# Unread identity products on TensorE ahead of the first weights and at eleven places of block 1

## The chip, the cores and the metric

One Trainium2 chip, of which the kernel uses one core. The metric is the device time of one execution in microseconds (us). PE is the tensor engine, DVE the vector engine, ACT the scalar engine, POOL the general engine (GpSimd), SP the engine that issues the transfers (DMAs).

## The reference

Two blocks in a row over one sequence of 256 tokens, model width 1024, in float32. The first:

```
def first_block(x, ...):
    h = rmsnorm(x, norm1_g)
    hp = h @ w_in
    y_ssm = s5_mixer(hp[..., :o1], ...)
    y_nsa = nsa_mixer(hp[..., o1:o2], hp[..., o2:o3], hp[..., o3:o4], ...)
    gate = sigmoid(hp[..., o4:].reshape(bsz, s, 2, 1024))
    merged = gate[..., 0, :] * (y_ssm @ w_proj_ssm) + gate[..., 1, :] * (y_nsa @ w_proj_nsa)
    x = x + merged @ w_out
    h2 = rmsnorm(x, norm2_g)
    return x + square(relu(h2 @ w_up)) @ w_down
```

`s5_mixer` is a diagonal complex recurrence of 32 groups of 16 channels with 64 states each, a skip term, GELU and a gated projection. `nsa_mixer` is attention of 8 heads of width 64 in 2 key groups, with three branches that gates add up: attention to keys and values of compressed blocks of 32 tokens, to selected blocks of 64, and to a window of 512. At 256 tokens the selection (16 blocks) and the window take in all earlier tokens. The second block has two layers, each a half-weighted gated feed-forward, a mixer (retention in the one, latent attention in the other, both with attention to a memory), and a feed-forward. The change touches the first block alone.

## The kernel before

The class `Prog` issues the program piece by piece on a tile framework. The framework gives out buffers, puts in the waits, and decides itself in which order the instructions of each engine stand; only an instruction given to `keep_in_program_order` keeps its place. So the order of the program's text is a wish, and a few more instructions at one place can move others elsewhere.

Activations lie transposed, 128 channels by 128 tokens, in two token tiles t = 0 and 1 (`xT`). Weights come from HBM in blocks of up to 1024 KB a transfer (`raw`), issued by SP. Most are split in two halves (`load`, L262 and L263): ACT rounds to `wh`, DVE subtracts to get `wl`, and three products of the fast kind (fp32r, one pass of the array) stand for one f32 product. Some matrices of block 1 (the inputs of the recurrence `u`, queries `q`, keys and values `kvb` and `kva`, the first quarter of the gates `mg`) are multiplied unsplit (`raw_proj`, L304) as f32, for which PE makes two passes: a count of x8 in the trace is four such products. Their blocks land in turn in the buffers named `raw`, `wh` and `wl`, so `mm<-wh,hTl` with eight in a group at the beginning is such a product, too.

`mm` (L222) issues every matrix product, `tr` (L226) every transpose, which is a product with the identity `idn`. All results land in eight banks: two called `tr`, two `mm`, and `acc0` to `acc3`. A new owner of a bank waits for the last reader of the one before.

Block 1 weaves four strands together (0 to about 185 us):

- `block1_proj` (L879 on), once per token tile: the projections above, and for q and k the norm of each head (`head_norm`: DVE sums up `nms` L854 and L855, POOL takes it to the power −1/2 as `nr` L332 and multiplies `q` L858), then transposes in `flip` (`u_rest`, `q_rest` L911, `c_rest` L931, `k_rest` L947). After them come the gates `mg`.
- the recurrence: `ssm_setup` makes its tables, among them `K0` by 32 small products of 32 columns; then eight steps `ssm_states` (L765 to L780): products of `uT` and `sB` into acc0 and acc1, four multiplications on DVE by the table `cst` (L765, into `ta` and `tb`), two sums (L766, L767), a scan (L775), a rotation back (L776, L777), and POOL's part (L779, L780). From the third step on POOL makes the table `cst` itself (`ssm_table`, L743 to L745). `ssm_out` multiplies the states by `sC`.
- the compressed attention: `compress`, which makes the compressed keys and values (`ph`, then `kc`) and the weights `PcT` of both token tiles (L1030 on).
- the heads: `nsa_pair` (L1060 on), one pair of heads c (g = 0 and 1) at a time: scores into acc2 and acc3, maximum and exponential (L1074, L1076), then the scaling `ns` by `nsm` (L1088 on DVE for t = 0, L1086 on ACT for t = 1), the transposes of `ns`, and a copy to `PT` (L1095), from which `nsa_values` makes the output.

Behind block 1's mixers come the feed-forward and the second block, which are large products from end to end.

Of the kernel before, what the change touches and what calls it, by code (L numbers as in the profile page):

```python
# [15 lines left out]
P = 128  # L16
# [161 lines left out]
class Prog:  # L178
# [42 lines left out]
    def mm(self, out, l, r, start, stop, **kw):  # L221
        self.nc.tensor.matmul(out, l, r, start=start, stop=stop, **kw)  # L222
# [73 lines left out]
    def raw_proj(self, out, name, n, hT):  # L296

        _, _, K, _, uk, un = MATS[name]
        nk = K // P
        for kb in range(nk // uk):  # L300
            w = self.raw_unit((name, n, kb))
            for k in range(uk):
                kk = kb * uk + k
                self.mm(out[:, :un], hT[:, kk], w[:, k, :], kk == 0, kk == nk - 1)  # L304
            yield
# [29 lines left out]
    def consts(self):  # L335
        nc, cp = self.nc, self.cp
        self.idn = self.sb(cp, [P, P], "idn")
        make_identity(nc, self.idn)
        self.mhalf = self.sb(cp, [P, 16], "mhalf")
# [231 lines left out]
    def ssm_setup(self, pool, np_):  # L571
        nc, v, g = self.nc, self.nc.vector, self.nc.gpsimd
# [9 lines left out]
        sp = sb([P, 48], "sp")  # L582
# [49 lines left out]
        g = nc.gpsimd  # L632
# [68 lines left out]
        pt = self.ps("tr")  # L701
        for i in range(4):
            for n in (0, 1):
                for jj in range(4):
                    j = 4 * i + jj
                    self.mm(pt[32 * jj:32 * jj + 32, 32 * i:32 * i + 32], bs[n][:, j, :], self.sC[:, 0, n, j, :], n == 0, n == 1, tile_position=(0, 32 * jj))
# [162 lines left out]
    def block1_proj(self, sp, pool, t):  # L869
# [16 lines left out]
        def flip(src, n):  # L886
            pt = self.ps("tr")
            for c in range(n):
                self.tr(pt[:, c * P:(c + 1) * P], src[:, c * P:(c + 1) * P])
            return pt  # L890
# [50 lines left out]
        def k_rest(k=k):  # L941
            pt = flip(k, 2)
# [21 lines left out]
    def compress(self, pool):  # L964
# [8 lines left out]
        ph = self.ps("tr")  # L973
        for o in range(16):
            for i in (0, 1):
                self.mm(ph[64 * i:64 * i + 48, :P], XT[i][:, o:o + 8 * 47 + 1:8], self.w1[i][:, o, :], o == 0, o == 15, tile_position=(0, 64 * i))
# [29 lines left out]
        pt = self.ps("tr")  # L1006
        self.tr(pt[:, :16], kc)
# [23 lines left out]
        for t in (0, 1):  # L1031
            pt = self.ps("tr")
            for c in range(4):
# [14 lines left out]
            pt2 = self.ps("tr")  # L1048
            self.tr(pt2[:, :P], s.rearrange("p h c -> p (h c)"))
            nc.scalar.copy(self.PcT[:, t * P:(t + 1) * P], pt2[:, :P])  # L1050

    def nsa_pair(self, pool, c, PTs):
# [9 lines left out]
        for t in (0, 1):  # L1062
            nk = P * (t + 1)
            sp = [self.ps(f"acc{2 + g}") for g in (0, 1)]
            sv = [x[:, :2 * nk].rearrange("p (b k) -> p b k", b=2) for x in sp]

# [11 lines left out]
        for g in (0, 1):  # L1078
# [3 lines left out]
            for t in (0, 1):  # L1082
# [6 lines left out]
                pt = self.ps("tr")  # L1089
                for b in (0, 1):  # L1090
# [576 lines left out]
```

## Time and profile before

| | |
|---|---|
| three runs | 1413.26, 1415.21, 1417.49 us; median 1415.21 |
| profiled execution | 1412.85 us, its span 1411.0 us |
| mean granted clock of PE in the span | 0.991 |
| PE busy | 1382.6 us, 98% of the span |
| DVE, ACT, POOL busy | 65%, 53%, 10% |
| bytes read from HBM | 236.39 MB, 168 GB/s over the span |
| chain that ended last | PE 85%, DVE 7%, ACT, POOL and issue 2% each |

The span is what the trace covers; the execution's own time is 1.85 us longer. The granted clock is 1.00 at PE's full 2.4 GHz and 0.50 at 1.2 GHz; a mean between says how a stretch was divided between the two. "Busy" counts from an instruction's start to its end, and matmuls overlap by their tails: of a group of matmuls the trace gives the start and the length to the last end, and the next group starts before that end. An entry in square brackets is idle time of the engine just before the group, and what ended it.

### The profile page before, as it was taken

The page shows a single profiled execution, that of the slowest core. Times are in us where ns is not written, and L with a number is a line of the kernel's source. Part 1 is how long each engine was busy: PE and PEld are TensorE (multiplying, and loading weights), DVE is VectorE, ACT ScalarE, POOL GpSimd, SP SyncE. Part 2 cuts the span into 40 slices and gives each one's busy share as a digit, 9 for nine tenths or more (in the row PEclk, how much of TensorE's full clock was granted, in tenths as well). Part 3 has the DMA queues.
Part 4 walks back from the last instruction along what each step waited for, and adds up shares of the span by engine and source line. Part 5 has one row for each costly group of instructions (what it writes and reads, how often), then busy time and mean ns, then how long its engine had stood idle before and what let it go on. Part 6 is the DMA issues. An engine that isn't in the chain of part 4 may idle for free.

```text
span 1411.0 us, 18497 instructions
## 1 busy us (share of the span) xinstructions
PE 1382.6 (98%) x6690; PEld 1111.1 (79%) x6690; DVE 911.7 (65%) x2030; ACT 749.3 (53%) x1647; POOL 135.8 (10%) x147
## 2 busy tenths in 40 slices
PE   8999999999999999999999999999999999999997
PEld 3556788888887888899877888888888887788886
DVE  6777687855677555577688565576555596865553
ACT  3335556544665444465376454465444586745442
POOL 2744100800000000011000000000000010000000
PEclk9998999999999999999999999999999999999999
DMA  9212355755555555335354555546555252565540
GB/s 359 89 65 75 128 190 176 259 183 181 188 194 181 185 194 186 134 124 190 131 183 164 190 198 197 187 149 209 181 192 194 74 188 76 194 215 197 184 150 30
DMA packets 39691, 238.63 MB, mean 169 GB/s; under 512 B 5808, under 2 KB 8112, under 8 KB 14000
## 3 DMA queue, kind: packets, MB, share of 16 engines
q1 hardware_dynamic: 39600, 237.45, 48.2%
q8 instruction: 52, 0.85, 0.2%
q14 instruction: 39, 0.32, 0.1%
HBM read 236.39 MB, written 1.05 MB: 168 GB/s over the span
## 4 chain that ended last, share of the span: by engine, by line
PE 85%; DVE 7%; ACT 2%; issue 2%; POOL 2%; DMA 1%; SPq 0%; POOLq 0%; DVEq 0%; ACTq 0%
PE mm L222 48%; PE acc L222 33%; PE tr L226 4%; DVE wl L263 2%; DMA raw<-in_wts_dram 1%; PE tr L222 1%; ACT wh L262 1%; DVE tb L775 1%; DVE xT L438 0%; POOL nr L332 0%; DVE ns L1074 0%; DVE ly L1502 0%; ACT hTh L395 0%; POOL lr L332 0%; POOL rr L332 0%
## 5 line engine op out<-in xcount | busy, mean ns | idle before, releaser
L263 DVE TENSOR_TENSOR wl<-raw,wh 128x512 fp32r<-128x512 f32 (+2 forms) x852 | 535.4, 678 | 258.8 <-ACT wh L262 258.0
L262 ACT CAST wh<-raw 128x512 fp32r<-128x512 f32 (+2 forms) x852 | 462.0, 606 | 303.7 <-PE mm L222 150.8
L222 PE MATMUL mm<-wh,hTl 128*128 128x512 f32 (+2 forms) x1056 | 406.8, 390 | 0.6 <-DVE hTl L396 0.6
L222 PE MATMUL mm<-wh,hTh 128*128 128x512 f32 (+2 forms) x1024 | 400.1, 391 | 1.9 <-ACT hTh L395 1.5
L222 PE MATMUL mm<-wl,hTh 128*128 128x512 f32 (+2 forms) x1024 | 395.0, 386 | 0.0
L222 PEld LDWEIGHTS mm<-wh,hTl 128*128 128x128 f32 x1056 | 199.5, 189 | 42.7 <-issue 3.9
L222 PEld LDWEIGHTS mm<-wh,hTh 128*128 128x128 f32 x1024 | 193.5, 189 | 42.8 <-ACT hTh L395 4.6
L222 PEld LDWEIGHTS mm<-wl,hTh 128*128 128x128 f32 x1024 | 193.9, 189 | 36.2 <-issue 0.7
L222 PE MATMUL acc<-wh,ffhh 128*128 128x512 f32 x480 | 196.4, 409 | 0.0
L222 PE MATMUL acc<-wh,ffhl 128*128 128x512 f32 x480 | 189.0, 394 | 0.0
L222 PE MATMUL acc<-wl,ffhh 128*128 128x512 f32 x480 | 188.7, 393 | 0.0
L460 ACT ACTIVATE ffs<-mm,rstd 128x256 f32<-128x256 f32 x88 | 41.7, 474 | 137.7 <-PE mm L222 135.1
L461 DVE SCALAR_TENSOR_TENSOR ffh<-mm,rstd,ffs 128x256 f32<-128x256 f32 x88 | 42.4, 482 | 105.1 <-ACT ffs L460 103.2
L222 PEld LDWEIGHTS acc<-wh,ffhl 128*128 128x128 f32 x480 | 90.2, 188 | 20.1
L222 PEld LDWEIGHTS acc<-wl,ffhh 128*128 128x128 f32 x480 | 90.6, 189 | 16.8
L222 PEld LDWEIGHTS acc<-wh,ffhh 128*128 128x128 f32 x480 | 90.3, 188 | 16.4
L332 POOL TENSOR_TENSOR rr<-ms,mhalf 128x1 f32<-128x1 f32 x12 | 6.9, 575 | 761.8 <-DVE ms L418 761.1
L222 PE MATMUL acc<-wh,mx 128*128 128x512 f32 x160 | 54.5, 404 | 0.0
L326 DVE TENSOR_TENSOR ffhl<-tr,ffhh 128x256 fp32r<-128x256 f32 (+1 forms) x104 | 47.7, 459 | 6.6 <-ACT ffhh L325 5.6
L325 ACT CAST ffhh<-tr 128x256 fp32r<-128x256 f32 (+1 forms) x104 | 41.7, 401 | 17.3 <-PE tr L226 17.3
L226 PEld LDWEIGHTS tr<-idn,ffh 128*128 128x128 f32 x240 | 32.2, 139 | 13.9 <-DVE ffh L461 0.6
L226 PE MATMUL tr<-idn,ffh 128*128 128x128 f32 x240 | 43.1, 272 | 0.0
(406 smaller groups left out, 1376.5 us busy)
## 6 DMA issues: line engine op xcount, KB each, us to landing
raw<-in_wts_dram SPq DMA_DIRECT2D x194, 1024.0 KB, 4.9
raw<-in_wts_dram SPq DMA_DIRECT2D x18, 768.0 KB, 4.2
raw<-in_wts_dram SPq DMA_DIRECT2D x4, 576.0 KB, 3.8
wl<-in_wts_dram SPq DMA_DIRECT2D x2, 1024.0 KB, 11.8
g8k<-in_cw_dram SPq DMA_DIRECT2D x2, 1024.0 KB, 10.0
wh<-in_wts_dram SPq DMA_DIRECT2D x2, 1024.0 KB, 9.1
memT<-in_memT_dram SPq DMA_DIRECT2D x4, 512.0 KB, 3.5
raw<-in_wts_dram SPq DMA_DIRECT2D x4, 256.0 KB, 5.1
```

Source lines behind the costliest of these rows:

```text
L222: self.nc.tensor.matmul(out, l, r, start=start, stop=stop, **kw)
L226: self.nc.tensor.transpose(out, src, self.idn[:n, :n])
L262: self.copies[key] = nc.scalar.copy(wh[:, s:s + h], raw[:, s:s + h]).ins
L263: self.subs[key] = nc.vector.tensor_sub(wl[:, s:s + h], raw[:, s:s + h], wh[:, s:s + h].bitcast(F32)).ins
L325: self.nc.scalar.copy(hi, src)
L326: self.nc.vector.tensor_sub(lo, src, hi.bitcast(F32))
L332: self.nc.gpsimd.tensor_tensor(r[:rows], ms, self.mhalf[:rows, :n], op=ALU.pow)
L460: nc.scalar.activation(s, pm[:, :256], AF.Silu, scale=rstd)
L461: nc.vector.scalar_tensor_tensor(h, pm[:, 256:], rstd, s, op0=ALU.mult, op1=ALU.mult)
L775: v.tensor_tensor_scan(fb[:, n], RD.rearrange("p j t -> p (j t)"), fa[:, n], 0.0, op0=ALU.mult, op1=ALU.add)
```

## The change

`mm` returns its instruction. A new method `warm(pt, n)` issues n products of the identity by itself, f32, 128 by 128, into the first 128 columns of a bank; nobody reads them, and the next product or transpose into the bank starts anew. It is called

- once in the constants with 11, before the first weights; the first `raw_proj` product is kept in program order (`began`), so that it stays behind them;
- in `ssm_setup` with 6, ahead of the products for `K0`;
- in `k_rest` of t = 0 with 8, ahead of the transposes of k;
- in `compress` with 3 ahead of `ph`, with 4 ahead of the transpose of `kc`, with 2 ahead of the scores of t = 1 and 3 ahead of the transpose of t = 0;
- in `nsa_pair` with 3 ahead of the first scores (c = 0, t = 0), and ahead of the transposes of t = 0 with 2 for c = 1, g = 0, with 8 for c = 1, g = 1, and with 2 for both g of c = 2.

That is 11 and 43, 54 in all. Each writes a bank that the place takes anyway, so no new bank is needed.

```diff
--- before.py
+++ after.py
@@ -219,7 +219,12 @@
             self.nc.gpsimd.dma_start(self.dbg[name], ap)
 
     def mm(self, out, l, r, start, stop, **kw):
-        self.nc.tensor.matmul(out, l, r, start=start, stop=stop, **kw)
+        return self.nc.tensor.matmul(out, l, r, start=start, stop=stop, **kw)
+
+    def warm(self, pt, n):
+
+        for _ in range(n):
+            self.mm(pt[:, :P], self.idn, self.idn, True, True)
 
     def tr(self, out, src):
         n = src.shape[0]
@@ -301,7 +306,10 @@
             w = self.raw_unit((name, n, kb))
             for k in range(uk):
                 kk = kb * uk + k
-                self.mm(out[:, :un], hT[:, kk], w[:, k, :], kk == 0, kk == nk - 1)
+                i = self.mm(out[:, :un], hT[:, kk], w[:, k, :], kk == 0, kk == nk - 1)
+                if not self.began:
+                    self.began = True
+                    self.tc.keep_in_program_order(i)
             yield
 
     def mm3(self, out, x, w, start, stop):
@@ -336,6 +344,8 @@
         nc, cp = self.nc, self.cp
         self.idn = self.sb(cp, [P, P], "idn")
         make_identity(nc, self.idn)
+        self.warm(self.ps("tr"), 11)
+        self.began = False
         self.mhalf = self.sb(cp, [P, 16], "mhalf")
         nc.vector.memset(self.mhalf, -0.5)
         self.ones = self.sb(cp, [P, 1], "ones")
@@ -699,6 +709,7 @@
         yield
 
         pt = self.ps("tr")
+        self.warm(pt, 6)
         for i in range(4):
             for n in (0, 1):
                 for jj in range(4):
@@ -883,8 +894,9 @@
         tok = slice(t * P, (t + 1) * P)
         todo = []
 
-        def flip(src, n):
+        def flip(src, n, warm=0):
             pt = self.ps("tr")
+            self.warm(pt, warm)
             for c in range(n):
                 self.tr(pt[:, c * P:(c + 1) * P], src[:, c * P:(c + 1) * P])
             return pt
@@ -939,7 +951,7 @@
         self.head_norm(pool, k, 4)
 
         def k_rest(k=k):
-            pt = flip(k, 2)
+            pt = flip(k, 2, 0 if t else 8)
             for c in range(2):
                 hi, lo = (y[:, c, tok] for y in self.kT)
                 x, gk = pt[:, c * P:(c + 1) * P], self.ngt[:, 2 + c:3 + c]
@@ -971,6 +983,7 @@
         H = sb([P, P], "s8", 2)
         v.memset(H, 0.0)
         ph = self.ps("tr")
+        self.warm(ph, 3)
         for o in range(16):
             for i in (0, 1):
                 self.mm(ph[64 * i:64 * i + 48, :P], XT[i][:, o:o + 8 * 47 + 1:8], self.w1[i][:, o, :], o == 0, o == 15, tile_position=(0, 64 * i))
@@ -1004,6 +1017,7 @@
         k3 = kc.rearrange("p (h d) -> p h d", h=2)
         v.tensor_mul(k3, k3, r.unsqueeze(2).to_broadcast([16, 2, 64]))
         pt = self.ps("tr")
+        self.warm(pt, 4)
         self.tr(pt[:, :16], kc)
         kcT = sb([P, 2, 16], "hk")
         v.memset(kcT, 0.0)
@@ -1030,6 +1044,7 @@
         self.PcT = sb([P, 256], "PcT")
         for t in (0, 1):
             pt = self.ps("tr")
+            self.warm(pt, 2 * t)
             for c in range(4):
                 self.mm3(pt[:, 32 * c:32 * c + 32], [x[:, c, t * P:(t + 1) * P] for x in self.qT], (kch, kcl), True, True)
             s = sb([P, 8, 16], "cs8", 1)
@@ -1046,6 +1061,7 @@
             v.scalar_tensor_tensor(sm.rearrange("p (c g) -> p c g", g=2), sm.rearrange("p (c g) -> p c g", g=2), vld[:, t:t + 1], gv, op0=ALU.mult, op1=ALU.mult)
             v.tensor_mul(s, s, sm.unsqueeze(2).to_broadcast([P, 8, 16]))
             pt2 = self.ps("tr")
+            self.warm(pt2, 0 if t else 3)
             self.tr(pt2[:, :P], s.rearrange("p h c -> p (h c)"))
             nc.scalar.copy(self.PcT[:, t * P:(t + 1) * P], pt2[:, :P])
 
@@ -1063,6 +1079,7 @@
             nk = P * (t + 1)
             sp = [self.ps(f"acc{2 + g}") for g in (0, 1)]
             sv = [x[:, :2 * nk].rearrange("p (b k) -> p b k", b=2) for x in sp]
+            self.warm(sp[0], 0 if c or t else 3)
 
             for n, (x, y) in enumerate(((0, 0), (0, 1), (1, 0))):
                 for g in (0, 1):
@@ -1087,6 +1104,8 @@
                 else:
                     v.tensor_mul(s, s, sm[g][:, t, :].unsqueeze(2).to_broadcast([P, 2, nk]))
                 pt = self.ps("tr")
+                if not t:
+                    self.warm(pt, {(1, 0): 2, (1, 1): 8, (2, 0): 2, (2, 1): 2}.get((c, g), 0))
                 for b in (0, 1):
                     for k in range(t + 1):
                         m = b * (t + 1) + k
```

The framework's order changes with it, on PE up to the end of the heads, on DVE and ACT in block 1; of SP's transfers the table `btab` and a few blocks of weights change places; POOL has one power moved. Three places matter here. In the rows the numbers behind the names are those of the buffers, which differ by a few between the two programs, and lines of the change are 5 to 17 higher (L226 became L231, L765 L776, L854 and L855 L865 and L866, L1088 L1105).

PE at the start of the program; `tr<-ones,s` sums the squares for the norm of the input. Before:

```order
L222 MATMUL mm_129<-raw_84,hTl_15_109 128x512
L222 MATMUL tr_123<-ones_74,s_16_119 128x1
L222 MATMUL mm_129<-raw_84,hTl_15_109 128x512 x3
L222 MATMUL mm_129<-wh_90,hTl_15_109 128x512 x4
L222 MATMUL tr_201<-ones_74,s_48_197 128x1
L222 MATMUL mm_207<-raw_84,hTl_47_187 128x512 x4
```

With the change:

```order
L222 MATMUL tr_72<-idn_67 128x128 x11
L222 MATMUL tr_135<-ones_86,s_17_131 128x1
L222 MATMUL mm_141<-raw_96,hTl_16_121 128x512 x4
L222 MATMUL mm_141<-wh_102,hTl_16_121 128x512 x4
L222 MATMUL tr_213<-ones_86,s_49_209 128x1
L222 MATMUL mm_219<-raw_96,hTl_48_199 128x512 x4
```

The eleven stand first. The product of `ones` and `s`, which stood between the first and the second product of the weights, now stands ahead of the first.

DVE where the norm of k of the first token tile (`nms`) is formed; `acc_137` and `acc_138` (before) are two banks of the states' products. Before:

```order
L765 TENSOR_TENSOR ta_646<-acc_137_636,cst_627 128x2x128
L765 TENSOR_TENSOR tb_647<-acc_137_636,cst_627 128x2x128
L765 TENSOR_TENSOR ta_646<-acc_138_637,cst_627 128x2x128
L765 TENSOR_TENSOR tb_647<-acc_138_637,cst_627 128x2x128
L639 TENSOR_TENSOR ta_655<-sC_407,small_154 128x512
L766 TENSOR_TENSOR ta_646<-ta_646,tb_647 128x256
L767 TENSOR_TENSOR ta_646<-ta_646,tb_647 128x256
L640 TENSOR_TENSOR sC_407<-sC_407,ta_655 128x512
L854 TENSOR_REDUCE nms_668<-ns_144_666 128x4
L639 TENSOR_TENSOR ta_659<-sC_407,small_154 128x512
L855 TENSOR_SCALAR nms_668<-nms_668 128x4
```

With the change:

```order
L776 TENSOR_TENSOR ta_667<-acc_138_657,cst_648 128x2x128
L776 TENSOR_TENSOR tb_668<-acc_138_657,cst_648 128x2x128
L649 TENSOR_TENSOR ta_676<-sC_419,small_166 128x512
L865 TENSOR_REDUCE nms_689<-ns_145_687 128x4
L650 TENSOR_TENSOR sC_419<-sC_419,ta_676 128x512
L866 TENSOR_SCALAR nms_689<-nms_689 128x4
L649 TENSOR_TENSOR ta_680<-sC_419,small_166 128x512
L650 TENSOR_TENSOR sC_419<-sC_419,ta_680 128x512
L268 TENSOR_TENSOR wl_765<-raw_763,wh_764 128x512 x2
L776 TENSOR_TENSOR ta_667<-acc_139_658,cst_648 128x2x128
L776 TENSOR_TENSOR tb_668<-acc_139_658,cst_648 128x2x128
```

The pair of multiplications of the second bank, and the two sums behind them, now stand behind `nms`; with the change two blocks of weights are subtracted ahead of that pair.

DVE in the second pair of heads (c = 1), where `ns` is scaled; `cst` is POOL's table for the next step of the states. Before:

```order
L1088 TENSOR_TENSOR ns_255_1134<-ns_255_1134,nsm_1121 128x256
L1081 TENSOR_TENSOR nsm_1125<-nsm_1125,gts_145 128x4
L776 TENSOR_TENSOR ta_1096<-tb_1097,cst_1077 128x512
L765 TENSOR_TENSOR ta_1250<-acc_271_1240,cst_1231 128x2x128
L765 TENSOR_TENSOR tb_1251<-acc_271_1240,cst_1231 128x2x128
L765 TENSOR_TENSOR ta_1250<-acc_272_1241,cst_1231 128x2x128
L765 TENSOR_TENSOR tb_1251<-acc_272_1241,cst_1231 128x2x128
L1088 TENSOR_TENSOR ns_256_1139<-ns_256_1139,nsm_1125 128x256
L766 TENSOR_TENSOR ta_1250<-ta_1250,tb_1251 128x256
L767 TENSOR_TENSOR ta_1250<-ta_1250,tb_1251 128x256
```

With the change:

```order
L1105 TENSOR_TENSOR ns_256_1175<-ns_256_1175,nsm_1162 128x256
L1097 RECIPROCAL nsm_1166<-nsm_1166 128x4
L788 TENSOR_TENSOR tb_1138<-tb_1138,cst_1118 128x512
L1098 TENSOR_TENSOR nsm_1166<-nsm_1166,gts_157 128x4
L1105 TENSOR_TENSOR ns_257_1180<-ns_257_1180,nsm_1166 128x256
L268 TENSOR_TENSOR wl_1392<-raw_1390,wh_1391 128x512 x3
L776 TENSOR_TENSOR ta_1293<-acc_272_1283,cst_1274 128x2x128
L776 TENSOR_TENSOR tb_1294<-acc_272_1283,cst_1274 128x2x128
L776 TENSOR_TENSOR ta_1293<-acc_273_1284,cst_1274 128x2x128
L776 TENSOR_TENSOR tb_1294<-acc_273_1284,cst_1274 128x2x128
```

The scaling of the second `ns` (`ns_256` before, `ns_257` with the change) stood behind the four multiplications by `cst` and now stands ahead of them. On PE its transposes have the eight identity products ahead of them, in the same bank:

```order
L222 MATMUL acc_272_1283<-uT_118,sB_169 128x128
L222 MATMUL acc_273_1284<-uT_118,sB_169 128x128
L222 MATMUL tr_1305<-idn_67 128x128 x8
L231 MATMUL tr_1305<-idn_67,ns_257_1180 128x128 x2
L231 MATMUL tr_1319<-idn_67,ns_261_1198 128x128 x4
```

## Rows read from the trace of the kernel before

**Rows 1.** Windows: busy us (instructions) per engine, TensorE clock, DMA share, GB/s.

```profile
50.00:60.00 10.00, 8.53 (x97) 4.80 (x96) 9.01 (x22) 3.98 (x11) 5.35 (x9) 0.83 0.01 2
90.00:100.00 10.00, 9.59 (x45) 7.50 (x43) 6.34 (x25) 3.63 (x11) 0.69 (x1) 0.66 0.09 37
110.00:120.00 10.00, 10.00 (x67) 7.32 (x66) 6.22 (x27) 4.38 (x16) 1.64 (x3) 0.68 0.14 30
130.00:140.00 10.00, 7.94 (x42) 5.30 (x41) 7.00 (x23) 5.14 (x16) 8.29 (x12) 0.83 0.00 0
100.00:160.00 60.00, 56.64 (x358) 39.84 (x357) 50.73 (x165) 36.28 (x114) 22.47 (x26) 0.91 0.26 86
200.00:1400.00 1200.00, 1193.45 (x5640) 985.16 (x5639) 760.51 (x1564) 653.82 (x1403) 67.59 (x61) 1.00 0.50 174
```

**Rows 2.** Waits of PE, first 200 us: line, releaser, total us, times, longest.

```profile
PE mm L222 <- DMA raw<-in_wts_dram: 7.0, 1, 7.0
PE tr L226 <- DVE ns L1088: 2.3, 2, 1.8
PE tr L226 <- POOL q L858: 1.7, 1, 1.7
...
PE tr L222 <- ACT XT L931: 0.5, 1, 0.5
PE acc L222 <- DVE tb L765: 0.4, 1, 0.4
PE tr L226 <- DVE cs L1047: 0.4, 1, 0.4
```

**Rows 3.** Timeline (start, us, instruction, idle before): PE, DVE, POOL, the start.

```profile
7.04 2.05 PE L222 MATMUL mm<-raw,hTl 128*128 128x512 f32 x2 [7.04 <-DMA raw<-in_wts_dram]
8.88 0.42 PE L222 MATMUL tr<-ones,s 128*128 128x1 f32 x2
...
12.55 3.60 PE L222 MATMUL mm<-wh,hTl 128*128 128x512 f32 x8
...
7.63 0.29 DVE L377 TENSOR_TENSOR s<-g8k 128x128 f32<-128x128 f32 x1
...
1.12 0.29 POOL masks.py:199 TENSOR_SCALAR_AFFINE_SELECT idn<-idn 128x128 f32<-128x128 f32 x1
```

**Rows 4.** Timeline of PE, about the K0 products.

```profile
53.12 0.76 PE L222 MATMUL tr<-sC,PT 128*32 128x32 f32 x64 [1.47 <-DVE qT L911]
...
54.91 5.40 PE L222 MATMUL acc<-wh,hTl 128*128 128x512 f32 x8
60.14 3.60 PE L222 MATMUL acc<-raw,hTl 128*128 128x512 f32 x8
63.57 0.82 PE L226 MATMUL tr<-idn,q 128*128 128x128 f32 x6
```

**Rows 5.** Timeline of PE, products of split weights in two stretches.

```profile
94.09 0.63 PE L222 MATMUL mm<-wh,hTl 128*128 128x512 f32 x1
94.52 0.63 PE L222 MATMUL mm<-wh,hTh 128*128 128x512 f32 x1
...
140.28 0.40 PE L222 MATMUL mm<-wh,hTh 128*128 128x512 f32 x1
140.52 0.39 PE L222 MATMUL mm<-wl,hTh 128*128 128x512 f32 x1
```

**Rows 6.** Timeline of PE and POOL, 70 to 81 us.

```profile
79.78 0.39 PE L222 MATMUL tr<-uT,K 128*128 128x128 f32 x2
80.10 1.08 PE L222 MATMUL tr<-X,sC 128*32 128x128 f32 x32
...
70.61 4.34 POOL L332 TENSOR_TENSOR nr<-nms,mhalf 128x4 f32<-128x4 f32 x1 [4.28 <-DVE nms L855]
```

**Rows 7.** Timeline of DVE and PE, 131 to 134 us.

```profile
131.45 0.42 DVE L765 TENSOR_TENSOR ta<-acc,cst 128x256 f32<-128x256 f32 x1 [1.78 <-POOL cst L745]
...
133.71 1.51 PE L226 MATMUL tr<-idn,ns 128*128 128x128 f32 x6 [1.84 <-DVE ns L1088]
```

## The prediction

> **What bounds the kernel now.** I read the stretches first, since one share of busy time hides what differs between them. From 200 to 1400 us PE is busy 1193.45 of 1200 us at a granted clock of 1.00 [rows 1]: nothing in the change touches that, and identity products there would only cost. All 54 go to block 1, before 200 us. There the stretches show four in which the clock was not full: 0.83, 0.66, 0.68 and 0.83 over ten us each [rows 1]. The clock has two levels, 1.2 and 2.4 GHz, so a mean of c is a share 2(1−c) of the time at 1.2: 3.4 + 6.8 + 6.4 + 3.4 = 20.0 us. Work that goes at half speed for 20.0 us would be done in 10.0, so **10.0 us** is the most that a better clock gives back here. Then the waits: in the first 200 us PE waits 7.0 us for the first weights, and after that for little: 2.3 for `ns`, 1.7 for `q`, 1.5 for `qT`, 0.5 for `XT`, 0.4 for `tb` and 0.4 for `cs` are what matters [rows 2, 4], 6.8 us together. So clock and waits can give this change some 17 us of 1412.85 at most, and the products' own time stands against that.
>
> What PE did before it fell is to be seen in two places: the clock is low just after the 1.47 us wait and the 64 small products at 53.12 [rows 4], and at the 1.84 us wait before 133.71 [rows 7].
>
> **The start (−0.8).** The 11 products need only the identity, ready on POOL at 1.12 + 0.29 = 1.4 us [rows 3], while PE stands idle until 7.04. One identity product is an f32 product, two passes of 128 columns. A pass of 512 columns at full clock takes 3.43/8 = 0.43 us (60.14 to 63.57, the row's 3.60 with its tail) [rows 4], so one of 128 takes 0.107 and a product 0.213 us, twice that at 1.2 GHz. Eleven take at most 4.7 us: over by 6.2, free, covered by the wait for the weights; without that cover they would cost 2.3 to 4.7.
> The order also moves: the product of `ones` and `s` now stands ahead of the first weights' product, which was at 7.04. It needs `s`, ready at 7.63 + 0.29 = 7.92 [rows 3], and takes some 0.3. So the eight passes start at 8.3 rather than 7.04: 1.3 us late. But before, the group lasted from 7.04 to 12.55, 5.5 us for 3.43 us of work at full clock (0.4 of it the `ones` product): the first two passes took 1.84 [rows 3], double time. At full clock the group now ends at 8.3 + 3.43 = 11.7, a gain of 0.8. Bounds: if PE is still at 1.2 GHz until 10.8, as it was, 2.5 us do 2.9 passes, 5.1 remain at 0.43, and it ends at 13.0: a loss of 0.5.
>
> **The slow stretches (−8.5).** That 1.2 GHz costs about half shows directly: eight passes of `hTl` by raw weights take 5.40 at 54.91 and 3.60 at 60.14, 1.8 lost [rows 4]; products of the split weights start 0.43 apart at 94.09 and 0.24 apart at 140.28 [rows 5]. Of the 10.0 us I take off 1.0, because in 130 to 140 PE was idle 2.06 us [rows 1], about half of which a faster clock doesn't shorten, and 0.5 for small products whose pace the columns may not set; that 0.5 is a choice. The bounds are 0 and −10.0. I take a value near the full one because the products sit at or just ahead of each of the four places: 6 at `K0` (53.12), 8 + 3 + 4 ahead of 92, 2 + 3 and 3 about the compressed attention and the first heads, 8 + 2 + 2 from the wait of 133.71 on. As far as identity products are PE work like any other, PE goes on without a hole.
>
> **The products' own time (+10.3).** Forty-three in block 1: 43 × 0.213 = 9.2, and 0.1 for the change-over at each of 11 places, 1.1. The nearest row of such a shape is `uT` by `K`, 128x128 in two passes: 79.78 to 80.10, 0.32 with its change-over [rows 6]. By it 43 would cost 13.8, the upper bound; 0.107 each, one pass, gives 4.6, the lower. The value between is taken because the products stand in rows of 2 to 8, in which the change-over is paid once.
>
> **The waits (−4.8).** Where a product needs no more than a free buffer, it runs inside the wait and its time, counted above, is given back. At `K0` it is not so: what PE waits for there is the release of the `tr` buffer by `qT` [rows 4], the identity products write that same buffer, and so come behind the 1.47 us, not in them. The 0.5 for `XT` is alike. Both stay. The `q` wait of 1.7 is a chain: POOL takes up its power when DVE has formed `nms`, 4.34 us from 70.61 [rows 6], and then scales `q`. In the new order two multiplications and two sums of the states, which stood ahead of `nms`, stand behind it, four instructions of about 0.4 as in [rows 7], and the chain starts some 1.6 earlier; what is left of the wait is filled by the 8 products. The `ns` wait of 1.84 is a queue: DVE's scaling of `ns` stood behind four multiplications that waited 1.78 us for POOL's table `cst` [rows 7], and now stands ahead of them. What is late next there is `cst` itself, for the states, and behind them the scan and its outputs: that is the second rival below. With `tb` and `cs`: 1.7 + 2.3 + 0.4 + 0.4 = 4.8. Bounds: 0, if each moves elsewhere, and −6.8, if `qT` and `XT` go too.
> ACT and SP get no instruction by the change; SP issues the table `btab` and a block of weights in another order, whose cover is that the DMA share in 100 to 160 is 0.26 [rows 1].
>
> **Sum:** −0.8 − 8.5 + 10.3 − 4.8 = −3.8; 1412.85 − 3.8 = **1409.0 us**. 1412.85 is the profiled execution, span 1411.0 us; the median of the runs shown is 1415.21, 2.4 above it. Against that median 1409.0 is 0.44% less, and 0.3%, 4.2 us, is about what a measurement of this kernel can tell from no change: faster means below 1411.0, slower above 1419.5.
>
> **The rivals.**
> *The clock stays low (the other side).* Identity products are almost all zeros; if they do not keep the clock at 2.4 GHz, the price is paid and nothing comes back. Start +0.5, slow stretches 0, products +10.3, waits −2.4 to −4.8: 1418.9 to 1421.2, say **1420**. It decides where less than 2 of the 8.5 us come back. For it: the stretches that fell did so although PE was busy 9.59 and 10.00 of 10 us in them [rows 1], so it isn't idleness alone that matters, and transposes against the same identity stand right by the fall. Against it: the first weights' products, slow at 7.04, did bring the clock up, and these are f32 products of the same kind. Chance 0.09.
> *DVE or POOL becomes the bound behind 100 us.* From 100 to 160 DVE is busy 50.73 of 60 and waits for POOL at 131 [rows 1, 7]. If the states and heads there end when they did, only what is won before 100 counts: start −0.8, slow stretches half (−4.3), 21 products +4.9, `q` and `tb` −2.1, together −2.3, and up to half of the 5.4 that the later products take comes on top, as they stand ahead of transposes that ACT and DVE wait for: 1410.5 to 1413.2, say **1412**. Against it: PE is busy 56.64 of those 60 [rows 1]. Chance 0.23.
> *A slow stretch stays, or comes at a new place.* Each kept stretch of 6.6 us gives back 3.3 less: 1412.3 with one, 1415.6 with two; say **1413**. For it: the new order alters what PE does before each. The Trainium skill ("TensorE: Matmul & The Clock Gate", Part 1) says that the place where one kernel's clock rises varies from run to run; the three runs shown, 1413.26 to 1417.49, agree with some such thing but don't show its cause. Chance 0.12.
> *No slow stretch here is the work of a wait.* The same page (section on HAM oscillation) ties the low clock to long waits for transfers between bursts of matmuls. The longest wait behind the start is 1.84 us, on DVE [rows 2, 7], so by that rule alone the change would fill nothing that matters and end near the first rival, 1420. The trace disagrees in so far as the clock fell in four stretches with only such waits; the measurement decides, and this adds nothing to the chance above.
>
> **Chances and range.** Forecast 0.50; first rival 0.09, second 0.23, third 0.12; better than forecast (below 1405, the slow stretches gone and products at the lower price) 0.06. Range **1404.5 to 1416.5**: it takes in the second and third rival and the lower price of the products, leaves out the first and half of what is better. Faster by over 0.3%: 0.46 of the forecast, 0.06, and a little of the second, **0.54**; within 0.3% **0.38**; slower **0.08**.
>
> **What would show it.** Right: granted clock 0.95 or more in 50 to 60, 90 to 100, 110 to 120 and 130 to 140; split-weight products 0.24 apart throughout; identity products 0.21 apart; the first weights' group over by 11.8 us; no PE wait for `q` or `ns` over 0.5; block 1 over about 3.8 us earlier and the rest unchanged. Wrong: a stretch below 0.9 behind the products, identity products 0.43 apart, DVE or POOL at the end of PE's waits between 100 and 160, or a difference behind 200 us.

## The result and the profile after

The change makes the kernel slower: 1428.63 us (median of 12 runs, 1419.00 to 1430.94) against 1415.45 (12 runs, 1411.15 to 1417.49), ratio 1.0084 with a 95% interval of 1.0069 to 1.0100. The forecast was 1409.0.

The profiled execution is one of the quickest, 1420.97 us (span 1419.1), so it tells only part of it. Each run also has its mean granted clock c: for the change from 0.996 down to 0.986, and nine of its 12 runs lie at 0.986 or 0.987. (1 − c) times the span is the time that 2.4 GHz throughout would give back at most; I call it **lost to the clock**. In the mean it is 15.7 us a run for the change (these 12 runs and 5 more) and 11.1 for before (17 runs taken beside the 5). The measure has one fault: the rows of the clock stand at 1.00 at the start whatever PE's pace, so the double time of before's first two passes (2.05 us, [rows 3]) isn't counted, while a fall behind the change's first products is. `start_only` below loses 2.8 us more than before by it, in the same time. `later_only`, without the start, loses 15.0 against 11.1 and is 11.5 us slower in the mean. So of some 12 to 13 us, 3 to 4 are clock and 8 to 9 are something else. The change was to win on the clock.

The windows that answer to [rows 1], of the profiled execution after, and 140 to 150 beside them (columns as there):

```profile
50.00:60.00 10.00, 8.27 (x112) 5.79 (x111) 7.62 (x20) 4.38 (x11) 5.09 (x8) 1.00 0.01 2
90.00:100.00 10.00, 8.62 (x77) 7.18 (x75) 8.09 (x26) 3.73 (x11) 0.69 (x1) 1.00 0.02 7
110.00:120.00 10.00, 8.13 (x69) 5.59 (x67) 8.04 (x25) 4.81 (x15) 2.66 (x4) 0.83 0.41 162
130.00:140.00 10.00, 7.54 (x70) 6.15 (x68) 9.33 (x17) 4.68 (x10) 6.98 (x8) 1.00 0.10 15
140.00:150.00 10.00, 8.59 (x36) 6.15 (x40) 5.76 (x26) 5.53 (x21) 1.42 (x2) 0.83 0.31 119
100.00:160.00 60.00, 53.85 (x373) 39.41 (x373) 50.06 (x151) 31.73 (x99) 20.50 (x24) 0.94 0.26 86
200.00:1400.00 1200.00, 1191.87 (x5628) 984.34 (x5627) 763.32 (x1569) 656.80 (x1408) 65.72 (x61) 1.00 0.50 175
```

The stretches at 50 and 90 are at 1.00, as was forecast; whether that is the products' work is asked below. But a new one is at 115, and the one of 133 has moved to 142. From 200 us on nothing has changed.

The waits of PE in the first 200 us after, which answer to [rows 2]:

```profile
PE mm L222 <- DVE yn L1136: 2.0, 1, 2.0
PE tr L222 <- DVE s L387: 2.0, 1, 2.0
PE tr L222 <- DVE qT L923: 1.9, 2, 1.6
PE tr L231 <- DVE cs L1062: 1.9, 1, 1.9
PE tr L222 <- ACT PT L1114: 1.8, 1, 1.8
...
PE tr L222 <- ACT s L1010: 1.4, 1, 1.4
PE acc L222 <- DVE nmn L1091: 0.4, 1, 0.4
```

Behind the start they come to 9.8 us, with 0.4 in rows of 0.2; before it was 7.5. `ns` (2.3) and `q` (1.7) are gone, as forecast. In their place stand `yn` 2.0, `cs` 1.9, `PT` 1.8 and `s` 1.4: other instructions of the same chains.

The start, to be laid beside [rows 3]:

```profile
1.46 4.86 PE L222 MATMUL tr<-idn 128*128 128x128 f32 x22 [1.46 <-POOL idn masks.py:199]
8.34 0.38 PE L222 MATMUL tr<-ones,s 128*128 128x1 f32 x2 [2.02 <-DVE s L387]
8.58 5.38 PE L222 MATMUL mm<-raw,hTl 128*128 128x512 f32 x8
13.79 3.60 PE L222 MATMUL mm<-wh,hTl 128*128 128x512 f32 x8
```

The second group of raw products starts at 13.79, not 12.55 as before. The 11 products take 4.86 us, then PE stands still for 2.02, and the weights' eight passes take 5.2 us again (8.58 to 13.79) where 3.43 was forecast. The clock, the last number but two in a row, was granted into the tenth microsecond and then fell, after the hole and not in it:

```profile
8.00:9.00 1.00, 0.67 (x3) 0.52 (x4) 0.28 (x1) 0.00 (x0) 0.00 (x0) 1.00 1.04 391
9.00:10.00 1.00, 1.00 (x3) 0.53 (x2) 0.00 (x0) 0.00 (x0) 0.00 (x0) 0.68 0.99 361
10.00:11.00 1.00, 1.00 (x2) 0.34 (x1) 0.00 (x0) 0.00 (x0) 0.00 (x0) 0.50 1.00 375
```

The place of the head c = 1, g = 1, which answers to [rows 7]; first PE, then ACT:

```profile
133.92 2.05 PE L222 MATMUL tr<-idn 128*128 128x128 f32 x16 [1.79 <-ACT PT L1114]
135.81 0.82 PE L231 MATMUL tr<-idn,ns 128*128 128x128 f32 x6
...
141.41 0.50 PE L222 MATMUL mm<-wh,hTh 128*128 128x512 f32 x1 [2.04 <-DVE yn L1136]
```

```profile
131.67 0.91 ACT L1103 ACTIVATE ns<-ns,nsm 128x256 f32<-128x256 f32 x2 [1.80 <-DVE nsm L1098]
132.48 1.12 ACT L267 CAST wh<-raw 128x512 fp32r<-128x512 f32 x2
133.51 0.84 ACT L1114 COPY PT<-tr 128x256 f32<-128x256 f32 x2
```

DVE's scaling of `ns` is early now, but PE waits as long, 1.79 us, for the bank: its last reader is ACT's copy `PT`, which stands behind ACT's scaling of other heads and two casts of weights, until 133.51. The eight products write that bank. They start when the wait is over, and take 1.89 us, 0.236 each. 2.04 us later comes the next wait: PE's gate products need a bank that DVE's copy `yn` still reads.

### The profile page after: what moved, and what is told of

It reads as the page before. It is cut to its first block, busy times and chain, and to the rows that moved or that the text cites. A ratio compares the mean times of both kernels' runs of the same rounds, so it can differ in the third digit from the quotient of the medians.

```text
span 1419.1 us, 18708 instructions
## 1 busy us (share of the span) xinstructions
PE 1390.5 (98%) x6798; PEld 1122.2 (79%) x6798; DVE 915.4 (65%) x2030; ACT 749.5 (53%) x1647; POOL 132.0 (9%) x147
## 4 chain that ended last, share of the span: by engine, by line
PE 86%; DVE 6%; ACT 3%; DMA 2%; issue 2%; POOL 1%; SPq 0%; POOLq 0%; DVEq 0%; ACTq 0%
PE mm L222 48%; PE acc L222 33%; PE tr L231 4%; DVE wl L268 2%; DMA raw<-in_wts_dram 2%; PE tr L222 1%; ACT wh L267 1%; DVE xT L448 0%; DVE tb L786 0%; DVE ly L1521 0%; ACT hTh L405 0%; POOL lr L340 0%; DMA xT<-in_xT_dram 0%; POOL rr L340 0%; DVE hTl L406 0%
## 5 line engine op out<-in xcount | busy, mean ns | idle before, releaser
L231 PEld LDWEIGHTS tr<-idn,ffh 128*128 128x128 f32 x240 | 32.2, 140 | 13.8 <-DVE ffh L471 0.6
L231 PE MATMUL tr<-idn,ffh 128*128 128x128 f32 x240 | 43.2, 272 | 0.0
```

The costliest lines, as they stand in the source:

```text
L231: self.nc.tensor.transpose(out, src, self.idn[:n, :n])
```

## The experiments

Runs of an experiment and of the kernel before were taken on the same chip. The table has, for each, the identity products in it, how many lines a text comparison of PE's order with before's adds or takes out (identity products not counted), the medians, the ratio with its interval, and what is lost to the clock in the mean run, its own and before's. A row that moved stands in that comparison at least twice, in some runs much oftener: at the fewest, about 80 rows of PE move in the change, 93 in compress_only, 66 in compress_ones, 65 in compress_no_p1, 55 in compress_no_kc, 25 in heads_only, 12 in k0_h11_free and 10 in order_kept.

| run | products | PE lines changed | us, before's | ratio (95%) | lost to the clock, before's |
|---|---|---|---|---|---|
| again (the change) | 54 | 356 | 1426.50, 1413.41 | 1.0094 (1.0074 to 1.0113) | 14.0, 11.1 |
| start_only | 11 | 2 | 1414.58, 1413.41 | 1.0000 (0.9979 to 1.0021) | 13.9, 11.1 |
| later_only | 43 | 354 | 1425.94, 1413.41 | 1.0087 (1.0060 to 1.0114) | 15.0, 11.1 |
| dense | 43 | as later_only | 1422.91, 1414.15 | 1.0072 (1.0048 to 1.0096) | 13.0, 10.2 |
| start_22 | 22 | 2 | 1416.94, 1414.15 | 1.0015 (0.9997 to 1.0032) | 11.3, 10.2 |
| no_h11 | 35 | 360 | 1421.08, 1414.15 | 1.0051 (1.0027 to 1.0075) | 11.4, 10.2 |
| order_kept | 13 | 50 | 1413.63, 1414.15 | 1.0001 (0.9988 to 1.0013) | 10.7, 10.2 |
| k0_same_bank | 6 | 0 | 1414.31, 1414.12 | 1.0000 (0.9986 to 1.0015) | 10.4, 11.3 |
| k0_free_bank | 6 | 0 | 1413.13, 1414.12 | 0.9988 (0.9970 to 1.0006) | 10.9, 11.3 |
| k0_free_again | 6 | 0 | 1409.71, 1413.26 | 0.9986 (0.9970 to 1.0002) | 7.9, 9.7 |
| compress_only | 15 | 232 | 1422.10, 1414.12 | 1.0049 (1.0031 to 1.0066) | 17.0, 11.3 |
| heads_only | 14 | 210 | 1417.42, 1414.12 | 1.0025 (1.0011 to 1.0039) | 12.2, 11.3 |
| compress_ones | 5 | 278 | 1423.74, 1414.35 | 1.0048 (1.0027 to 1.0069) | 16.3, 11.6 |
| compress_ones_again | 5 | 278 | 1419.44, 1413.26 | 1.0061 (1.0040 to 1.0083) | 13.3, 9.7 |
| compress_no_kc | 11 | 156 | 1414.34, 1414.35 | 0.9996 (0.9985 to 1.0006) | 12.0, 11.6 |
| compress_no_p1 | 13 | 154 | 1418.16, 1414.35 | 1.0031 (1.0019 to 1.0043) | 15.0, 11.6 |
| k0_h11_free | 13 | 24 | 1413.81, 1414.35 | 0.9994 (0.9975 to 1.0014) | 9.5, 11.6 |

### Start or later places

`again` is the change itself. `start_only` takes the 43 out, `later_only` the 11:

```diff
-        self.warm(self.ps("tr"), 11)
-        self.began = False
+        self.began = True
```

> The changed kernel as it is, once more. Two groups of times are seen in its runs, about 1420 at a mean granted clock of 0.995 and about 1429 at 0.987; the one trace so far is of the first. Theory A (the first weights' products lose the clock): a run of the second group has its low clock in the first 50 us. Theory B (the later places): it has it between 50 and 200 us. Both expect the median within 0.2% of 1428.6, ratio 1.007 to 1.010.

> The kernel before with the 11 products at the start and the kept place of the first weights' product, none of the 43. The order is the one before but for the product of ones and s, which stands ahead of the weights. Theory A: it bears most of the loss, 8 us or more over before (ratio 1.006 or more). Theory B: only what the trace of the change shows at the start, +1.25 us (ratio 1.000 to 1.002).

> The changed kernel without the 11 at the start and with the first product free; the 43 and the new order of block 1 stay. Theory A: within 3 us of before (ratio 0.999 to 1.002). Theory B: 8 to 12 us over before (ratio 1.006 to 1.009), with waits of PE in 90 to 150 us of 7 us or more.

The later places bear nearly all of it; theory A fell. `start_only` is even with before, within 3 us either way. The second trace of the change, of a run of 1426.59 us, shows where a slower run loses its time:

```profile
90.00:100.00 10.00, 8.54 (x62) 6.48 (x60) 6.78 (x21) 3.15 (x8) 0.69 (x1) 0.84 0.14 57
100.00:110.00 10.00, 10.00 (x41) 9.16 (x42) 5.50 (x20) 1.81 (x7) 0.00 (x0) 0.50 0.00 0
110.00:120.00 10.00, 9.72 (x21) 5.34 (x21) 5.40 (x15) 2.26 (x7) 5.92 (x8) 0.64 0.39 131
```

From 96.7 to 117.2 us, 20.5 us on end, PE is at 1.2 GHz, and it is busy throughout: 10.00 of 10 us at 0.50. That is no hole.

### Whether zeros are to blame

```diff
-            self.mm(pt[:, :P], self.idn, self.idn, True, True)
+            self.mm(pt[:, :P], self.xT[0][:, 0, :], self.xT[0][:, 0, :], True, True)
```

> The run later_only with the 43 products taken of a block of the input (dense numbers) in place of the identity; the order of all engines is that of later_only. Theory Z (products that are nearly all zeros do not keep the clock up): the slow stretches between 90 and 150 us go, mean clock 0.995 or more, median 6 us or more below later_only's 1425.9. Theory Q (the products take their time and the waits only move, whatever the data): the same as later_only within 3 us, clock 0.985 to 0.992 in most runs.

Ratio 1.0072 against later_only's 1.0087, the intervals overlap; its trace has 1.2 GHz for 13.7 us from 92.9 and again from 116.8. Theory Z, by which the median had to lie 6 us or more below later_only's, fell: dense numbers do not keep the clock up either. A gain of 2 or 3 us by them is not excluded.

### The start, filled

`start_only` with 22 in place of 11.

> start_only with 22 products ahead of the first weights in place of 11, so that PE is at work until about 8.2 us, when the product of ones and s can go. If it was the hole of 2.4 us behind the 11 that let the clock fall again, the first weights' product now goes at 2.4 GHz: eight passes of raw in 3.5 us instead of 5.0, the first group over by 12.0 us instead of 13.4, the median 1 to 2 us below start_only's 1414.6. If the clock's fall has another reason, the group takes 5 us or more as in start_only.

```profile
1.46 7.17 PE L222 MATMUL tr<-idn 128*128 128x128 f32 x44 [1.46 <-POOL idn masks.py:199]
9.16 0.38 PE L222 MATMUL tr<-ones,s 128*128 128x1 f32 x2 [0.52 <-DVE s L387]
9.40 3.68 PE L222 MATMUL mm<-raw,hTl 128*128 128x512 f32 x8
12.92 3.60 PE L222 MATMUL mm<-wh,hTl 128*128 128x512 f32 x8
```

The clock half came true: 44 passes take 7.17 us, where all at 1.2 GHz would take 44 × 0.213 = 9.4, so it rose during them, and with a hole of 0.52 behind them in place of 2.0 to 2.7, the weights' eight passes take 3.52 us (9.40 to 12.92). The time half did not: `s` came at 9.16 in this run, and the group is over at 12.92, later than before's 12.55. Against before, the ratio is 1.0015, not below start_only's 1.0000; the intervals overlap.

### A product in the wait, and behind it

`k0_same_bank` keeps the six products at K0 as the change has them, `k0_free_bank` gives them another bank:

```diff
+        self.warm(self.ps("acc3"), 6)
         pt = self.ps("tr")
-        self.warm(pt, 6)
```

> The kernel before with the six products at K0 alone, in the bank tr as in the change; the order on PE is exactly that of before. Theory Q (they come behind the release of their bank): the wait of 1.47 us stays, the products add 6 x 0.26 = 1.5 us, the slow stretch at 55 to 58.6 goes (-1.8 us): K0's products start at 54.6 to 54.9 and the group of raw products that was at 60.14 starts within 0.5 us of that. Rival (they fill the wait): K0's products start at 53.1, that group at 58.4. Median within 1 us of before for Q, 1.8 below for the rival.

> As k0_same_bank, but the six products go to a bank that nobody uses just then (acc3); the order on PE is again that of before, and they wait for nothing. Theory Q: now they run in the wait, from 51.7 to 53.1; K0's products start at 53.1 as before, the slow stretch at 55 goes, the group of raw products starts at 58.4, 1.7 us earlier than before; median 1 to 2 us below before. If a product that fills a wait does not keep the clock up: the group stays at 60.1.

> k0_free_bank once more, for its interval. By its trace (K0's wait filled, the stretch at 55 gone): 1.6 us below before, ratio 0.9988. If its first result was luck of the clock: 1.000.

PE at that place, same bank:

```profile
54.10 1.60 PE L222 MATMUL tr<-idn 128*128 128x128 f32 x12 [1.57 <-DVE qT L922]
55.64 0.76 PE L222 MATMUL tr<-sC,PT 128*32 128x32 f32 x64
...
60.96 3.60 PE L222 MATMUL acc<-raw,hTl 128*128 128x512 f32 x8
```

and free bank:

```profile
51.68 1.50 PE L222 MATMUL acc<-idn 128*128 128x128 f32 x12
53.41 0.76 PE L222 MATMUL tr<-sC,PT 128*32 128x32 f32 x64 [0.23 <-DVE qT L922]
...
58.73 3.60 PE L222 MATMUL acc<-raw,hTl 128*128 128x512 f32 x8
```

PE's order is that of before in both, to the row. In the same bank the wait of 1.57 stands ahead of the six, they cost 1.54 (54.10 to 55.64), the slow stretch is gone (the raw group follows K0's products by 5.3 us, 7.0 before), and the group starts at 60.96: 0.8 later than in [rows 4], all of which came from ahead of this place, since PE got to the wait 0.9 later (54.10 − 1.57 = 52.53, before 53.12 − 1.47 = 51.65). So products and stretch cancel. In the free bank they run from 51.68 in the wait, of which 0.23 is left, and the group starts at 58.73. Theory Q holds as to where the products run. That they are what takes the slow stretch at 55 away isn't shown: of the nine traces without products at K0 three have it (before, start_only, heads_only) and six do not, five of them (compress_only and those like it, below) with before's order on PE up to this place. compress_ones, where before took 5.40 us for the second row:

```profile
54.09 0.76 PE L222 MATMUL tr<-sC,PT 128*32 128x32 f32 x64 [1.48 <-DVE qT L921]
55.87 3.70 PE L222 MATMUL acc<-wh,hTl 128*128 128x512 f32 x8
```

Both sets of 12 runs of the free bank put it 0.12% and 0.14% below before, each with an interval that just reaches 1. Taken together (24 runs against 49) the means differ by 1.9 us, with a standard error of 0.8; that the other bank beats the same bank in time isn't shown by the intervals, only in the traces. It is the one version here that is probably faster than both kernels.

`no_h11` leaves out the eight at the head c = 1, g = 1 (`(1, 1): 8` out of the table):

> later_only without the eight products ahead of the transposes of the second head of c = 1; its order on PE is later_only's but for 24 rows. Theory Q (they come behind the release of their bank, not in the wait): PE still waits 1.5 to 2 us at that place for ACT's copy PT, then goes on with the transposes, and block 1 gets 2.0 us shorter. Rival (they fill a wait that is there anyway): the wait grows to 3.5 to 4 us and the time does not change.

```profile
PE tr L231 <- ACT PT L1113: 2.8, 2, 1.8
```

The wait for `PT` at that place is still 1.79 us, it did not grow, and the transposes follow at once; the wait for `yn` behind it is gone, too. Over before's mean the mean run is 4.1 us less than later_only's (7.3 against 11.5), of which 2.7 is less lost to the clock. The two traces have 17.1 us of 1.2 GHz each ahead of 200 us, and behind the mixers one and the same product (`acc<-wl,mTh`) starts at 228.5 against 231.0, 2.5 us earlier, near the 2.0 of theory Q. So the eight filled nothing.

`k0_h11_free` adds seven products ahead of those transposes, in the bank acc0, to k0_free_bank:

```diff
+                if not t and (c, g) == (1, 1):
+                    self.warm(self.ps("acc0"), 7)
                 pt = self.ps("tr")
```

> k0_free_bank, and seven products ahead of the transposes of the second head of c = 1, in acc0, which is free then; the order on PE stays that of before but for 24 rows. Theory Q (a product pays where it runs inside a wait): the waits for qT and ns (1.5 and 1.8 us) are filled, the slow stretches at 55 and at 133 go: -1.7 for each, ratio 0.9965 to 0.9985. If the products only shift the slow stretches: ratio 0.999 to 1.001.

```profile
135.14 2.30 PE L222 MATMUL acc<-idn 128*128 128x128 f32 x14 [2.56 <-DVE tb L775]
```

acc0 was not free: the products wait 2.56 us for DVE's `tb`, more than the 1.84 that they were to fill. No gain beyond K0's, for the same reason as in the change.

### Products or order

`compress_only` and `heads_only` keep one group of places each, `order_kept` K0, `ph` and the two heads of c = 2.

> The kernel before with 13 of the 43 products (6 at K0, 3 at ph, 2 and 2 at c = 2), chosen because the order on PE stays nearly that of before. If the new order is what makes the change slow, this one is within 2 us of before or faster, as the slow stretch at 55 to 58.6 goes (-1.8) against 13 x 0.25 = 3.2 of products: +1.4 us, ratio 1.000 to 1.002, and the other slow stretches stay as before. If the products bring the loss, a share of 13 in 43 of 12.5 us: +3.8 us, ratio 1.0027.

> Of the 43 only the 15 at the compressed attention (ph 3, kc 4, scores 2, transpose 3, first scores of the heads 3); block 1's order changes in 232 rows of PE. If the loss goes with the products: 15 x 0.25 = 3.8 us over before, ratio 1.0027. If it goes with the new order at this place (waits for cs and s of the compressed attention, 3.2 us in the change): 5 us or more over before, ratio 1.004 or more.

> Of the 43 only the 14 ahead of the transposes of the heads; 210 rows of PE change. By the products: 14 x 0.25 = 3.5 us over before, less what the wait for ns gives back (1.8 if filled), ratio 1.001 to 1.0025. If the waits for PT and yn (1.8 and 2.0 us in the change) come from here, they stand in this run too, and the ratio is 1.004 or more.

Thirteen products with the order nearly kept cost nothing (1.0001). The compressed attention's 15 cost 8 us, as the expectation by the new order had it (5 us or more; 3.8 by the products). The heads' 14 cost some 3.3 to 4, what the products alone would; in their trace `yn` waits 3.5 us and `PT` only 0.2. The two together are nearly later_only's 12. The window of compress_only and pieces of its PE timeline there:

```profile
100.00:110.00 10.00, 10.00 (x38) 8.45 (x38) 4.50 (x15) 1.40 (x5) 0.00 (x0) 0.50 0.00 0
```

```profile
94.37 1.65 PE L222 MATMUL acc<-idn 128*128 128x128 f32 x6
...
99.77 2.51 PE L222 MATMUL tr<-kc,qT 128*128 128x32 f32 x11
102.11 1.20 PE L222 MATMUL tr<-idn 128*128 128x128 f32 x4
...
103.97 1.22 PE L222 MATMUL tr<-idn 128*128 128x128 f32 x4
104.84 2.72 PE L222 MATMUL tr<-kc,qT 128*128 128x32 f32 x12
...
108.64 0.79 PE L222 MATMUL mm<-wl,hTh 128*128 128x512 f32 x1
```

Much of that stretch, 91.8 to 112.3 us, is small work: 12 + 12 score products of 32 columns, identity products, few large ones; before, 12 gate products of 512 columns stood between the first product of the compressed keys and the last scores, in this order 4. The clock came back at 112, behind eight of them in a row from 108.64. That made a guess, theory L: the slow stretch gets long where the order moves the large products away. Three runs tried it, with fewer products at the same places:

```diff
compress_ones:   ph 1, kc 1, scores 1, transpose 1, first scores 1
compress_no_kc:  ph 3,       scores 2, transpose 3, first scores 3
compress_no_p1:  ph 3, kc 4,           transpose 3, first scores 3
```

> compress_only with one product at each of its five places in place of 3, 4, 2, 3, 3. The order of block 1 changes in 278 rows of PE against before, but 11 of the 12 large products (512 columns, split weights) still stand between the first product of the compressed keys and the last scores kc by qT; compress_only has 4 there. Theory L (the clock comes back where the large products run without a break, and the new order takes them away): no slow stretch over 7 us there, time lost to the clock 10 to 11 us as before, ratio 0.999 to 1.002. Rival (any new order here costs it): a stretch of over 12 us, ratio 1.003 or more.

> compress_only without the four products ahead of the transpose of kc: 11 products, 11 large products left between the small ones. Theory L: no slow stretch over 7 us there, 11 x 0.25 = 2.8 us for the products, ratio 1.000 to 1.003. Theory of the products (the loss goes with their number): 11 of 15 of 7.7 us, ratio 1.004.

> compress_only without the two products ahead of the scores of t = 1: 13 products, but only 4 large products left between the small ones, as in compress_only. Theory L: the slow stretch of 15 us or more from about 92 us is there as in compress_only, ratio 1.004 to 1.006. Otherwise it is as short as in compress_no_kc.

> compress_ones once more. Most of its runs have a mean clock of 0.986, some 20 us lost to it, against 10 before. If the order around the compressed attention is what loses it, the trace shows slow stretches of 15 us or more in sum between 88 and 125 us; if it is elsewhere, the stretch from 88 to 125 has at most 10 us of 1.2 GHz, as the first trace of it and before have.

Five products cost some 8 us, eleven nothing, thirteen 4. So the loss doesn't go with the number of products, and not with every new order, since compress_no_kc's is new as well: what is left is which order the framework finds. Theory L agrees with compress_no_kc and with compress_no_p1 (its trace has 1.2 GHz for 20.5 us from 89.6) but not with compress_ones, which keeps 11 of the 12 large products and loses as much. Its two traces fell on milder runs (9.5 and 11.6 us lost to the clock, 16.3 in the mean of the first set) and don't show where the usual run loses it; the second has 10.2 us of 1.2 GHz between 88 and 125 us, which by the sign given beforehand doesn't speak for that place. The wait for `yn` is no answer either. compress_ones, then compress_no_kc, which waits longer and loses nothing:

```profile
PE mm L222 <- DVE yn L1134: 3.0, 1, 3.0
PE mm L222 <- DVE yn L1133: 4.0, 1, 4.0
```

The order alone doesn't settle the clock of a run. k0_free_again and k0_h11_free have one and the same order on PE up to about 130 us, that of before, with the six products at K0. Behind the start, the rows of the first show no 1.2 GHz at all up to 127 us, those of the second 23.9 us of it by 120, 13.7 of them on end from 91.9, with all 12 gate products inside, which is against theory L. First k0_free_again, then k0_h11_free:

```profile
90.00:100.00 10.00, 9.14 (x50) 6.69 (x49) 7.87 (x32) 4.95 (x17) 0.69 (x1) 1.00 0.01 2
100.00:110.00 10.00, 9.63 (x55) 6.55 (x54) 10.00 (x35) 5.00 (x16) 6.88 (x8) 1.00 0.42 144
90.00:100.00 10.00, 9.58 (x40) 7.45 (x38) 6.08 (x24) 3.63 (x11) 0.69 (x1) 0.59 0.01 2
100.00:110.00 10.00, 10.00 (x39) 6.25 (x39) 7.65 (x24) 3.39 (x13) 3.68 (x4) 0.72 0.13 28
```

So a slow stretch of one trace can't be put down to its order; only the mean over runs can (compress_only's five runs all have 0.988, before's beside them 0.988 to 0.998). The three stretches of 20.5 us (again, compress_only, compress_no_p1) begin in, or up to 1.8 us behind, PE's wait of 1.45 to 1.49 us for `s`; but the change's first trace has that wait too (1.4) and no fall. What exactly keeps the clock low stays open.

## Why the prediction was wrong

- **The slow stretches (−8.5): the step that failed.** "PE goes on without a hole" was taken from the places of the products in the order of before, and 1.2 GHz was to go with it. The stretch at 55 is gone in every trace with products at K0, as forecast, but also in six of the nine without. Of the others, the change's first trace kept two of 3.4 us (at 115 and 142), the second 20.5 us on end from 96.7, with PE busy all the while: against 20.5 us before, the one gave back 6.8 us, the other nothing. In the mean of the runs the time lost to the clock rose by 3 to 4 us. That the new order brings 1.2 GHz back is argued from the means of the runs; why, is open. That a stretch may "come at a new place" was the third rival, with 3.3 us each and a chance of 0.12; it missed that a stretch may also be three times as long with PE busy in it.
- **The waits (−4.8): wrong in sign, the second step that failed.** 7.5 us became 9.8, and 8.4 in the second trace. The step was "where a product needs no more than a free buffer, it runs inside the wait". It was checked for K0 and `XT`, where the text says that the products come behind, and not for the heads and the compressed attention, where it is the same: `PT` 1.8 and `s` 1.4 are releases of the products' own bank. For `ns` the prediction looked at DVE's queue alone; ACT's queue, with two casts ahead of the copy, was late next, and then DVE's `yn`.
- **The products (+10.3): right.** 0.257 each at K0 with the change-over, 0.236 at the head, so 43 come to 10.1 to 11.1.
- **The start (−0.8): +1.24 in the first trace, +2.75 in the second** (its second group starts at 15.30), beyond the bound of +0.5. The sum took the clock as up once the 11 had run and as staying up. Behind the hole that the new wait for `s` made it fell again: at 9.4 us in the first trace, 0.8 us after the weights' products had begun, and at 8.0, in the hole, in `again` and start_only. With a hole of 0.5 us, in start_22's trace, it did not. In the time of all runs no effect of the start is shown (start_only 1.0000, 0.9979 to 1.0021).
- **The sum.** With what the traces show in place of the forecast terms, start, slow stretches behind it, products and waits: +1.2 − 6.8 + 10.3 + 2.3 = +7.0 in the first trace and +2.8 + 0 + 10.3 + 0.9 = +14.0 in the second. Their spans are 8.1 and 13.8 us longer than before's, so little is left out. In a run like the first, the price of the products and the waits make the loss; in nine of the first 12 runs, at 0.986 or 0.987, the clock gives nothing back either.
- **The first rival** had the side, and its condition (less than 2 of the 8.5 us come back) holds in those nine runs; but its 1420 is 8.6 below the median, and its reason was zeros in the operands, against which `dense` speaks. **The second** was half there: PE's new waits are for DVE and ACT, though not as a bound on the whole stretch, since DVE's busy time from 100 to 160 hardly moved (50.73 to 50.06).
- **The page's rule** (the Trainium skill, "TensorE: Matmul & The Clock Gate", section on HAM oscillation), which ties the low clock to waits for transfers between bursts, gave about 1420, nearer than the forecast. The trace still disagrees with its ground: the clock stays low over 20 us in which PE has no hole at all.
- The range leaves room for the rivals, not for a spread from run to run: the three runs shown before differ by 4 us, the change's by 12.

## What to carry to other kernels

An instruction that fills a wait must not need what the wait is for: look up what releases its buffer before it is counted as free, and give it one that is idle (K0: in the same bank the wait stayed and nothing was gained; in another the wait was filled, and the mean was 1.9 us lower, with a standard error of 0.8). Where a scheduler decides the order, a few unread instructions are a new order first and work second: 5 products cost some 8 us where they moved the order, 13 nothing where it nearly stayed, so compare the order on every engine, and prefer places where it does not move. A clock that varies from run to run is judged by many runs' clocks; the first trace of this change had the clock at 0.995, and nine of its first 12 runs had 0.986 or 0.987. One trace shows one run: from 20 to 120 us the same order had 0 us of 1.2 GHz in one trace and 23.9 in another.

## What the runs showed of the hardware

- PE can stay at 1.2 GHz for 20.5 us while it is busy 10.00 of 10 us, with products of 512 columns among its work (again, compress_only; in compress_no_p1 with 0.85 us idle at its beginning).
- The same order on PE can have, behind the start, no 1.2 GHz up to 127 us (k0_free_again) or 23.9 us of it by 120 (k0_h11_free).
- The clock rose during one unbroken run of 22 identity products (start_22: 44 passes in 7.17 us), and a hole of 2.0 to 2.7 us behind 11 of them was followed by 1.2 GHz, in the hole or 0.8 us after it (again, start_only; the change).
- The rows of the granted clock show 1.00 at the start, though products go at double time there (before: two passes of 512 columns in 2.05 us at 7.04).
- One kernel's runs with identical instructions spread by 12 us with their mean clock (the change: 0.996 at 1419.00, 0.986 at 1430.94).
